# Loading w_ada's columns three steps ahead of their sums in the first pass of an encoder layer

## Chip, cores and metric

The kernel runs on one core of a Trainium2 chip. The metric is the device time of one execution in microseconds (us), lower is better; the median of the runs is compared.

## What is computed

One layer of a gated encoder, 1024 rows by 2048 columns, all in float32:

```python
mod = silu(c) @ w_ada + b_ada                    # w_ada: 2048 x 6144
shift, scale, gate = split(mod, 3)
h = rmsnorm(x, pre_g) * (1 + scale) + shift
q, k, v, gate_a, u, gate_p = split(h @ w_in)     # w_in: 2048 x 4608
y_a = windowed_gqa(q, k, v) * silu(gate_a)
y_p = multiscale_pool(u) * silu(gate_p)
g_a, g_p = split(sigmoid(h @ w_merge + b_merge)) # w_merge: 2048 x 4096
merged = g_a * (y_a @ w_br_attn) + g_p * (y_p @ w_br_pool)
out = x + gate * rmsnorm(merged @ w_out, post_g)
```

The change is about `mod`: a product of one row with a 2048 x 6144 matrix: 50 MB of loads and little arithmetic.

## The kernel before

**The big products.** A column pair is 256 columns of `w_in` or `w_merge`. It is worked out by a seven-product Strassen scheme in `strassen`, with each operand split into a high and a low part (`split`: ScalarE writes `whi`, VectorE writes `wlo`). One product is 12 matmuls of 128x512 on TensorE. The contraction has two halves, so there are two passes over all 34 pairs; the first pass, which the change touches, covers the half of `h` that is made first and stores its partial results in `part_d`.

**Order inside a pair.** `run` puts the last product of a pair behind the second product of the next one. So TensorE's order over a pair is: X (moving operand B11), V (T3), then the last product of the pair before (Z, B22), then Z (T2), X (B21), V (T4), Z (T1). X and V have one PSUM bank each of the tag "mm"; V's bank is read by VectorE after T4 (`finish("21", ...)`, the row `u<-V`), and the next pair's T3 product writes the same bank. The four results of a pair are stored as `c` (block 12 of the pair before, in the middle of the pair), `c` (block 11), `u` (block 21) and `p` (block 22).

**Weights.** Two raw tiles of 512 KB per pair (`load_raws`, line 187; four buffers). The first holds a11 and a21, the second a12 and a22. VectorE makes `ws` = a11 - a21 (L105), then a21 + a22 (`raw<-raw,raw`, L102) and further sums. The low parts `wlo` are ready up to four products ahead, because there are four buffers.

**Side work in the first pass.** The stretch of 22 pairs under `pass1(n1, side, EASY, ...)` carries steps of a deque `side`, alternately four and three steps a pair. In them are the columns 4 to 7 of shift and scale (`modulation_steps`: 32 steps with two 256 KB loads of `w_ada` and two sums on VectorE each, and four closing steps) and then the 32 steps of the gate (`gate_step`: one 512 KB load into a tile shown as `gada`, and one sum into `gacc`). The tiles share a pool `xa` of five buffers. From pair 11 on, `weight_sums` is laid over the same pairs: four loads of `w_out` (tiles `sw`), four sums on VectorE, four stores to `ws_dS`.

**What sets the order.** A scheduler orders each engine's instructions by its own estimates of time, except where `keep` (`keep_in_program_order`) pins an instruction behind the one that was written before it for the same engine. The sums of `weigh` are pinned on VectorE. Every load and store of this stretch goes through SyncE's queue (SP) in one fixed order, and an entry that waits holds up all behind it.

Of the kernel before, what the change touches and what calls it, by code (L numbers as in the profile page):

```python
# [12 lines left out]
F32 = mybir.dt.float32  # L13
# [7 lines left out]
P = 128  # L21
S = 1024
D = 2048
KT = D // P
# [18 lines left out]
def encoder_layer(ctx: ExitStack, tc: tile.TileContext, x, c, table, w_ada, b_ada, pre_g,  # L43
# [18 lines left out]
    w_ada, w_in, w_pg, w_ba, w_bp, w_merge, w_out = (  # L62
        w[0] for w in (w_ada, w_in, w_pg, w_ba, w_bp, w_merge, w_out))

    def pool(name, bufs=1, **kw):
        return tc.tile_pool(name=name, bufs=bufs, reuse_waits="tile", **kw)
# [9 lines left out]
    def uid(s):  # L76
        cnt[0] += 1
        return f"{s}_{cnt[0]}"

    def bank(tag, name="b"):  # L80
        return psum.tile([P, 512], F32, tag=tag, name=uid(name), bufs=1 if tag in SEEDED else 2)
# [8 lines left out]
    def keep(ins):  # L90

        tc.keep_in_program_order(ins)
# [14 lines left out]
    load = nc.sync.dma_start  # L107
# [233 lines left out]
    xa = mid.enter_context(pool("xa", 5))  # L341
# [8 lines left out]
    for r0, src in ((0, c[0]), (16, b_ada[0, 0:D]), (32, b_ada[0, D:2 * D]),  # L350
                    (48, pre_g[0]), (64, b_merge[0]), (96, pool_scale[0])):
        n = src.shape[0] // P
# [60 lines left out]
    def ada_tile(j, q):  # L413
        at = xa.tile([P, 2, 4, P], F32, tag="xa", name=uid("ada"))
        for kk in range(2):
            r0 = (2 * q + kk) * P
            load(at[:, kk].rearrange("p (g h) n -> p g (h n)", g=2), w_ada[r0:r0 + P, 0:2 * D].rearrange("p (g n) -> p g n", g=2)
                 [:, :, j * 256:(j + 1) * 256])
        return at

    def sum_columns(acc):
        pm = bank("at", "PM")
        for g in range(4):
            nc.tensor.matmul(pm[:, g:g + 1], acc[:, g, :], ones, start=True, stop=True)
        return pm

    def mod_columns(j, pm):
        tc.keep_in_program_order(nc.vector.tensor_tensor(
            modc[:, :, :, j], pm[:, 0:4].rearrange("p (g h) -> p g h", g=2),
            cols[:, 16:48].rearrange("p (g k) -> p g k", g=2)[:, :, 2 * j:2 * j + 2], ALU.add))  # L430
        nc.vector.scalar_tensor_tensor(modc[:, 1, :, j], modc[:, 1, :, j], 1.0,
                                       cols[:, 48 + 2 * j:50 + 2 * j], op0=ALU.add, op1=ALU.mult)

    def ada_slots(j):
        tiles = []
        for kc in range(KT):
            tiles.append(slot("ada", F32, (P, 4, P)))
            load(tiles[kc].rearrange("p (g h) n -> p g (h n)", g=2),
                 w_ada[kc * P:(kc + 1) * P, 0:2 * D].rearrange("p (g n) -> p g n", g=2)
                 [:, :, j * 256:(j + 1) * 256])  # L440
        return tiles

    def modulation(j, tile_of, pin=False):

        st_ = {}

        def step(q):
            if q == 0:
                st_["pv"] = bank("at", "GEMV")
            pv = st_["pv"]  # L450
            for kc in (2 * q, 2 * q + 1):
                g = kc % 4 * 32
                ins = nc.tensor.matmul(pv[g:g + 32, :], scz[:, kc, :], tile_of(kc), start=kc < 4,  # L453
                                       stop=kc >= 12, tile_position=(0, g))
                if pin:
                    tc.keep_in_program_order(ins)
            if q == 7:
                acc = xa2.tile([P, 4, P], F32, tag="acc", name=uid("acc"), bufs=2)
                tc.keep_in_program_order(
                    nc.scalar.activation(acc, pv.rearrange("p (g n) -> p g n", g=4), AF.Copy))  # L460
                mod_columns(j, sum_columns(acc))

        return [lambda q=q: step(q) for q in range(8)]

    def weigh(acc, t, kc):

        if kc == 0:
            ins = nc.vector.tensor_scalar(acc, t, sc[:, 0:1], None, op0=ALU.mult)
        else:
            ins = nc.vector.scalar_tensor_tensor(acc, t, sc[:, kc:kc + 1], acc,  # L470
                                                 op0=ALU.mult, op1=ALU.add)
        tc.keep_in_program_order(ins)

    def modulation_steps(j):

        st_ = {}

        def step(q):
            if q == 0:
                st_["acc"] = xa2.tile([P, 4, P], F32, tag="acc", name=uid("acc"), bufs=2)  # L480
            if q == 8:
                mod_columns(j, st_["pm"])
                return
            acc = st_["acc"]
            at = ada_tile(j, q)
            for kk in range(2):
                kc = q * 2 + kk
                weigh(acc, at[:, kk], kc)
            if q == 7:
                st_["pm"] = sum_columns(acc)  # L490

        return [lambda q=q: step(q) for q in range(9)]

    def modulate(eng, t, k):
        j, kh = k // 2, k % 2
# [43 lines left out]
    ada = [ada_slots(0), ada_slots(1)]  # L539
# [11 lines left out]
    side = deque(modulation(2, ada[2].__getitem__, True) + modulation(3, tile3, True))  # L551
# [98 lines left out]
    gp = gate_ctx.enter_context(pool("gatep"))  # L650
    gacc = gp.tile([P, D], F32, name="gacc")

    def gate_step(kc, q):
        qs = slice(q * 1024, (q + 1) * 1024)
        at = xa.tile([P, 1024], F32, tag="xa", name=uid("gada"))
        load(at, w_ada[kc * P:(kc + 1) * P, 2 * D + q * 1024:2 * D + (q + 1) * 1024])
        weigh(gacc[:, qs], at, kc)

    tab = gp.tile([33, NH], F32, name="tab")

# [16 lines left out]
    def gate_columns(n):  # L677
# [16 lines left out]
        else:  # L694
# [6 lines left out]
            nc.scalar.activation(rows, pt[0:KT, 0:P], AF.Copy)  # L701
            store(pg_d.rearrange("o (k p) -> (o k) p", p=P), rows)

    side = deque(s_ for j in range(4, 8) for s_ in modulation_steps(j))
    side.extend(lambda kc=kc, q=q: gate_step(kc, q) for q in range(2) for kc in range(KT))
    side.append(bias_lines)
    side.extend(lambda n=n: gate_columns(n) for n in range(6))
    EASY = ((0, 2, 4, 6), (1, 3, 5))
# [24 lines left out]
    h = {k: [sp.tile([P, 512], F32, name=f"h{k}_{s}") for s in range(2)] for k in PART[1]}  # L733
# [18 lines left out]
    def x_step(n):  # L752
        if n < 2 * NB:
            held[n] = fetch_x(n // 2, n % 2)
        if n >= 2:
            turn_x((n - 2) // 2, n % 2, held.pop(n - 2))

    side = deque(lambda n=n: x_step(n) for n in range(2 * NB + 2))
# [17 lines left out]
    side = deque()  # L776
# [12 lines left out]
    with pool("attn") as ap:  # L789
# [19 lines left out]
        qraw, q, bt, g, pr, pv = {}, {}, {}, {}, {}, {}  # L809
# [230 lines left out]
    for b, w in enumerate((w_ba, w_bp)):  # L1040
# [43 lines left out]
        for i in range(8):  # L1084
# [24 lines left out]
            at = [(n, open_gate) for n in (0, 1, 2, 3)] if i == 0 else []  # L1109
# [175 lines left out]
    side = deque()  # L1285
# [123 lines left out]
```

## Time and profile before

| | us |
|---|---|
| median of three runs | 2145.62 |
| the runs | 2143.08, 2147.35, 2145.62 |
| profiled execution, its own time | 2142.59 |
| its span | 2140.8 |
| TensorE busy in the span | 2096.1 (98%) |
| VectorE busy | 1537.3 (72%) |
| ScalarE busy | 1129.5 (53%) |

The stretch of the first pass with the side steps runs from about 152 us to about 565 us of the span. Times in the timeline rows are counted from the start of the span; a bracket at the end of a row is the idle time of the engine before it and what ended it.

### The profile page before, as it was taken

What the parts mean: (1) busy time and instruction counts of PE and PEld (TensorE: products, weight loads), DVE (VectorE), ACT (ScalarE), POOL (GpSimd) and SP (SyncE); (2) the same over time, 40 slices, a digit from 0 to 9 for tenths busy, and PEclk for the clock granted to TensorE, in tenths of its full rate; (3) what the DMA queues carried; (4) which work ended last, traced back from release to release, by engine and by line L of the source; (5) the groups of instructions that cost most, each with busy time, mean ns of one, the idle gap of its engine ahead of it and who ended that gap; (6) DMA issues with size and microseconds to landing.
All of it is one profiled execution on the core that took longest, in us unless ns stands there. A gap on an engine that the chain in (4) does not pass through costs nothing.

```text
span 2140.8 us, 28950 instructions
## 1 busy us (share of the span) xinstructions
PE 2096.1 (98%) x9567; PEld 1715.2 (80%) x9567; DVE 1537.3 (72%) x2754; ACT 1129.5 (53%) x2124; POOL 7.4 (0%) x66
## 2 busy tenths in 40 slices
PE   6999999999999999999999999999999999999998
PEld 4588888887878888888888888888788888778886
DVE  5786666777547676777776788666956977879667
ACT  5654444443474546767775433333645644667654
POOL 0000000000000000000000000000000000000000
PEclk9999999999999999999999999999999999999999
DMA  9986566898766356445454766765655655696996
GB/s 331 292 277 202 188 207 202 305 315 270 237 216 213 122 169 207 157 156 197 150 165 154 235 214 203 242 193 171 228 170 166 213 192 164 219 298 219 303 306 240
DMA packets 303255, 466.11 MB, mean 218 GB/s; under 512 B 23882, under 2 KB 144866, under 8 KB 303104
## 3 DMA queue, kind: packets, MB, share of 16 engines
q1 hardware_dynamic: 301648, 462.02, 65.6%
q0 software_dynamic: 1120, 2.19, 0.3%
q8 instruction: 75, 1.23, 0.2%
q14 instruction: 76, 0.62, 0.1%
q10 hardware_dynamic: 336, 0.06, 0.0%
HBM read 340.41 MB, written 125.85 MB: 218 GB/s over the span
## 4 chain that ended last, share of the span: by engine, by line
PE 80%; DMA 8%; DVE 7%; issue 2%; ACT 2%; SPq 0%; ACTq 0%; DVEq 0%
PE Z L235 26%; PE V L235 18%; PE X L235 17%; PE Z L1139 2%; PE Z L1141 2%; PE Z L1140 2%; DVE wlo L96 2%; DMA raw<-in_w_merge_dram 1%; PE V L1141 1%; PE V L1139 1%; PE V L1140 1%; PE X L1141 1%; PE X L1140 1%; PE X L1139 1%; PE GEMV L453 1%
## 5 line engine op out<-in xcount | busy, mean ns | idle before, releaser
L95 ACT ACTIVATE whi<-raw 128x512 fp32r<-128x512 f32 (+1 forms) x528 | 319.7, 609 | 504.5 <-PE Z L235 252.6
L96 DVE TENSOR_TENSOR wlo<-raw,whi 128x512 fp32r<-128x512 f32 (+1 forms) x528 | 346.6, 662 | 189.8 <-PE Z L235 116.5
L96 DVE TENSOR_TENSOR wlo<-wr,whi 128x512 fp32r<-128x512 f32 x224 | 151.1, 689 | 60.9 <-ACT whi L95 58.5
L95 ACT ACTIVATE whi<-wr 128x512 fp32r<-128x512 f32 x224 | 138.5, 629 | 92.8 <-DVE wlo L96 35.9
L102 DVE TENSOR_TENSOR raw<-raw,raw 128x512 f32<-128x512 f32 x80 | 55.2, 690 | 94.2 <-DMA raw<-in_w_merge_dram 70.8
L1078 ACT ACTIVATE gt<-gt,cols 128x512 f32<-128x512 f32 x64 | 46.1, 722 | 96.2 <-DMA gt<-proj_d 77.8
L235 PE MATMUL V<-T3h,whi 128*128 128x512 f32 x336 | 92.9, 396 | 3.3 <-DVE u L102 3.3
L235 PE MATMUL X<-B11h,whi 128*128 128x512 f32 x336 | 92.4, 393 | 1.7 <-DVE part L102 0.9
L235 PE MATMUL Z<-B22h,whi 128*128 128x512 f32 x336 | 92.4, 395 | 0.8 <-ACT u L290 0.8
L235 PE MATMUL V<-T4h,whi 128*128 128x512 f32 x336 | 92.0, 393 | 0.4 <-ACT T4h L95 0.4
L235 PE MATMUL Z<-T1h,whi 128*128 128x512 f32 x336 | 91.8, 392 | 0.3 <-ACT T1h L95 0.3
L235 PE MATMUL V<-T3l,whi 128*128 128x512 f32 x336 | 91.5, 392 | 0.0
L235 PE MATMUL Z<-T1l,whi 128*128 128x512 f32 x336 | 91.1, 390 | 0.2
L235 PE MATMUL X<-B11l,whi 128*128 128x512 f32 x336 | 91.1, 390 | 0.2 <-DVE B11l L96 0.2
L235 PE MATMUL Z<-T2h,whi 128*128 128x512 f32 x336 | 91.2, 392 | 0.0
L235 PE MATMUL V<-T4l,whi 128*128 128x512 f32 x336 | 91.0, 390 | 0.0
L235 PE MATMUL X<-B21h,whi 128*128 128x512 f32 x336 | 90.9, 391 | 0.0
L235 PE MATMUL V<-T4h,wlo 128*128 128x512 f32 x336 | 90.8, 390 | 0.0
L235 PE MATMUL Z<-B22l,whi 128*128 128x512 f32 x336 | 90.8, 390 | 0.0
L235 PE MATMUL Z<-T1h,wlo 128*128 128x512 f32 x336 | 90.8, 390 | 0.0
L235 PE MATMUL Z<-T2l,whi 128*128 128x512 f32 x336 | 90.7, 390 | 0.0
L235 PE MATMUL V<-T3h,wlo 128*128 128x512 f32 x336 | 90.6, 390 | 0.0
(306 smaller groups left out, 4847.0 us busy)
## 6 DMA issues: line engine op xcount, KB each, us to landing
part<-part_d SPq DMA_DIRECT2D x136, 256.0 KB, 4.8
ada<-in_w_ada_dram SPq DMA_DIRECT2D x128, 256.0 KB, 4.7
raw<-in_w_in_dram SPq DMA_DIRECT2D x64, 512.0 KB, 4.1
raw<-in_w_merge_dram SPq DMA_DIRECT2D x64, 512.0 KB, 5.7
wr<-ws_dS SPq DMA_DIRECT2D x64, 512.0 KB, 5.3
wr<-in_w_out_dram SPq DMA_DIRECT2D x48, 512.0 KB, 5.0
proj_d<-part SPq DMA_DIRECT2D x68, 256.0 KB, 2.2
sw<-in_w_out_dram SPq DMA_DIRECT2D x64, 256.0 KB, 5.4
```

Source lines behind the costliest of these rows:

```text
L95: ins = (nc.scalar.activation(hi, src, AF.Copy), nc.vector.tensor_tensor(lo, src, f32(hi), ALU.subtract))
L96: nc.vector.tensor_tensor(lo, src, f32(hi), ALU.subtract))
L102: return (eng or nc.vector).tensor_tensor(o, a, b, ALU.add)
L235: nc.tensor.matmul(ps, w_[:, i], op[mov][j][m_], start=fresh and i == 0 and n == 0, stop=i == nj - 1 and n == 2, skip_group_check=True)
L453: ins = nc.tensor.matmul(pv[g:g + 32, :], scz[:, kc, :], tile_of(kc), start=kc < 4, stop=kc >= 12, tile_position=(0, g))
L1078: nc.scalar.activation(gt, gt, AF.Sigmoid, bias=cols[:, col:col + 1])
L1139: nc.tensor.matmul(pb, hi, w[0], start=first, stop=False, skip_group_check=True)
L1140: nc.tensor.matmul(pb, lo, w[0], start=False, stop=False, skip_group_check=True)
L1141: nc.tensor.matmul(pb, hi, w[1], start=False, stop=last, skip_group_check=True)
```

## The change

Each side step of `w_ada` is split into a load and a sum. Step n first does the sum of unit n - 3 and then issues the load of unit n. The 32 + 32 units run through without closing steps of their own (the closing of a column is put ahead of the sum that comes then), so the deque is 74 steps long in place of 75; both make 22 pairs. The loads are pinned with `keep`, the five buffers stay.

```diff
-        def step(q):
+        def load_(q):
+            st_[q] = xa.tile([P, 2, 4, P], F32, tag="xa", name=uid("ada"))
+            for kk in range(2):
+                r0 = (2 * q + kk) * P
+                keep(load(st_[q][:, kk].rearrange("p (g h) n -> p g (h n)", g=2),
+                          w_ada[r0:r0 + P, 0:2 * D].rearrange("p (g n) -> p g n", g=2)
+                          [:, :, j * 256:(j + 1) * 256]))
+
+        def sum_(q):
...
-            acc = st_["acc"]
-            at = ada_tile(j, q)
+            at = st_.pop(q)
             for kk in range(2):
-                kc = q * 2 + kk
-                weigh(acc, at[:, kk], kc)
+                weigh(st_["acc"], at[:, kk], 2 * q + kk)
...
-    def gate_step(kc, q):
-        qs = slice(q * 1024, (q + 1) * 1024)
-        at = xa.tile([P, 1024], F32, tag="xa", name=uid("gada"))
-        load(at, w_ada[kc * P:(kc + 1) * P, 2 * D + q * 1024:2 * D + (q + 1) * 1024])
-        weigh(gacc[:, qs], at, kc)
+    def gate_sum(kc, q):
+        st_ = {}
+
+        def load_():
+            st_["at"] = xa.tile([P, 1024], F32, tag="xa", name=uid("gada"))
+            keep(load(st_["at"], w_ada[kc * P:(kc + 1) * P, 2 * D + q * 1024:2 * D + (q + 1) * 1024]))
+
+        return load_, lambda: weigh(gacc[:, q * 1024:(q + 1) * 1024], st_["at"], kc)
...
-    side = deque(s_ for j in range(4, 8) for s_ in modulation_steps(j))
-    side.extend(lambda kc=kc, q=q: gate_step(kc, q) for q in range(2) for kc in range(KT))
+    AHEAD = 3
+    units, then = [], {}
+    for j in range(4, 8):
+        sums_of, columns = ada_sums(j)
+        units += sums_of
+        then[len(units)] = columns
+    units += [gate_sum(kc, q) for q in range(2) for kc in range(KT)]
+
+    def unit_step(n):
+        m = n - AHEAD
+        if m in then:
+            then[m]()
+        if m >= 0:
+            units[m][1]()
+        if n < len(units):
+            units[n][0]()
+
+    side = deque(lambda n=n: unit_step(n) for n in range(len(units) + AHEAD))
```

The scheduler makes a new order of it on every engine. The first place is late in the gate's steps, on SP, ahead of the first raw tile of the pair that begins at 521 us in the profile before. In the names, `c` is a partial result on its way to `part_d`, `raw` a raw weight tile, `sw` and `ws_dS` belong to the weight sums. Before:

```order
L656 DMA gada_4567<-in_w_ada_dram 128x1024
L656 DMA gada_4610<-in_w_ada_dram 128x1024
L656 DMA gada_4661<-in_w_ada_dram 128x1024
L656 DMA gada_4716<-in_w_ada_dram 128x1024
L311 DMA part_d<-c_4487 128x512
L187 DMA raw_4657<-in_w_merge_dram 128x4x256
L656 DMA gada_4757<-in_w_ada_dram 128x1024
L311 DMA part_d<-c_4545 128x512
```

And after, ahead of the first raw tile of the same pair (here `raw_4666`):

```order
L661 DMA gada_4430<-in_w_ada_dram 128x1024
L661 DMA gada_4478<-in_w_ada_dram 128x1024
L187 DMA raw_4505<-in_w_merge_dram 128x4x256
L636 DMA sw_4527<-in_w_out_dram 128x512
L636 DMA sw_4529<-in_w_out_dram 128x512
L636 DMA sw_4531<-in_w_out_dram 128x512
L311 DMA part_d<-c_4496 128x512
L636 DMA sw_4533<-in_w_out_dram 128x512
L661 DMA gada_4536<-in_w_ada_dram 128x1024
L187 DMA raw_4666<-in_w_merge_dram 128x4x256
```

Four gate loads in a row have become one or two at a time.

The second place is VectorE around the read of V's bank (`u<-V`) at the same point. Before, the difference `ws` of the following pair, which needs its first raw tile, stands ahead of that read:

```order
L96 TENSOR_TENSOR wlo_4616<-ws_4613,whi_4615 128x512
L105 TENSOR_TENSOR sw_4520<-sw_4518,sw_4520 128x512
L105 TENSOR_TENSOR ws_4780<-raw_4657 128x512
L105 TENSOR_TENSOR sw_4633<-sw_4522,sw_4520 128x512
L102 TENSOR_TENSOR sw_4518<-sw_4518,sw_4633 128x512
L102 TENSOR_TENSOR u_964_4516<-V_4425,u_964_4516 128x512
L470 TENSOR_SCALAR gacc<-gada_4567,sc,gacc 128x1024
```

After, that difference comes eight rows behind the read, and all four weight sums stand ahead of it:

```order
L96 TENSOR_TENSOR wlo_4625<-ws_4622,whi_4624 128x512
L105 TENSOR_TENSOR sw_4529<-sw_4527,sw_4529 128x512
L105 TENSOR_TENSOR sw_4642<-sw_4531,sw_4529 128x512
L102 TENSOR_TENSOR sw_4527<-sw_4527,sw_4642 128x512
L105 TENSOR_TENSOR sw_4533<-sw_4533,sw_4642 128x512
L102 TENSOR_TENSOR u_968_4525<-V_4434,u_968_4525 128x512
L470 TENSOR_SCALAR gacc<-gada_4430,sc,gacc 128x1024
L96 TENSOR_TENSOR wlo_4648<-raw_4343,whi_4647 128x512
```

The wait for a raw tile has left the rows ahead of the read; a wait for the weight sums' loads may stand there instead.

The third place is SP two pairs earlier, where the four loads of a weight-sum unit are issued. Before, all four are ahead of the store of block 12:

```order
L633 DMA sw_4157<-in_w_out_dram 128x512
L633 DMA sw_4159<-in_w_out_dram 128x512
L633 DMA sw_4161<-in_w_out_dram 128x512
L633 DMA sw_4163<-in_w_out_dram 128x512
L656 DMA gada_4336<-in_w_ada_dram 128x1024
L311 DMA part_d<-c_4154 128x512
L187 DMA raw_4332<-in_w_merge_dram 128x4x256
```

After, three of them are behind it:

```order
L661 DMA gada_4145<-in_w_ada_dram 128x1024
L636 DMA sw_4166<-in_w_out_dram 128x512
L311 DMA part_d<-c_4163 128x512
L636 DMA sw_4168<-in_w_out_dram 128x512
L636 DMA sw_4170<-in_w_out_dram 128x512
L636 DMA sw_4172<-in_w_out_dram 128x512
L661 DMA gada_4199<-in_w_ada_dram 128x1024
```

The loads of the weight sums have moved back by up to a store; the four sums that use them stand ahead of `u<-V` on VectorE there too.

More of the change, by code (lines that the diff above doesn't have):

```diff
@@ L472, in weigh, with ada_sums @@
         tc.keep_in_program_order(ins)
-    def modulation_steps(j):
+    def ada_sums(j):
         st_ = {}
-        def step(q):
+        def load_(q):
[6 more added lines that the diff above has]
+        def sum_(q):
             if q == 0:
                 st_["acc"] = xa2.tile([P, 4, P], F32, tag="acc", name=uid("acc"), bufs=2)
-            if q == 8:
-                mod_columns(j, st_["pm"])
-                return
-            acc = st_["acc"]
-            at = ada_tile(j, q)
+            at = st_.pop(q)
             for kk in range(2):
-                kc = q * 2 + kk
-                weigh(acc, at[:, kk], kc)
+                weigh(st_["acc"], at[:, kk], 2 * q + kk)
             if q == 7:
-                st_["pm"] = sum_columns(acc)
-        return [lambda q=q: step(q) for q in range(9)]
+                st_["pm"] = sum_columns(st_["acc"])
+        return [(lambda q=q: load_(q), lambda q=q: sum_(q)) for q in range(8)], lambda: mod_columns(j, st_["pm"])
     def modulate(eng, t, k):
```

## The prediction

> **What bounds the kernel now.** I read the page's first part, then the stretch table for this pass, then TensorE's waits in it.
>
> ```profile
> span 2140.8 us, 28950 instructions
> PE 2096.1 (98%) x9567; PEld 1715.2 (80%) x9567; DVE 1537.3 (72%) x2754; ACT 1129.5 (53%) x2124; POOL 7.4 (0%) x66
> ```
>
> TensorE is busy in 98% of the span, so the change can only bring what TensorE loses in the stretch that it touches. The stretch table (busy us and count for each engine, then granted clock, share of the DMA engines, GB/s) and TensorE's waits between 140 and 570 us:
>
> ```profile
> 100.00:150.00 50.00, 50.00 (x222) 41.42 (x221) 42.54 (x91) 30.28 (x65) 0.10 (x1) 1.00 0.85 282
> 400.00:510.00 110.00, 107.54 (x469) 88.58 (x468) 82.71 (x116) 43.96 (x73) 0.00 (x0) 0.98 0.90 305
> PE V L235 <- DVE u L102: 2.5, 1, 2.5
> ```
>
> One wait in the whole stretch: a T3 product waits until VectorE has read V's bank. Its neighbourhood on TensorE (start, duration, instruction; the first rows of three pairs and the T3 product of two):
>
> ```profile
> 478.97 1.07 PE L235 MATMUL X<-B11h,whi 128*128 128x512 f32 x4
> 481.69 0.62 PE L235 MATMUL V<-T3h,whi 128*128 128x512 f32 x2
> ...
> 498.01 1.07 PE L235 MATMUL X<-B11h,whi 128*128 128x512 f32 x4
> 503.35 2.08 PE L235 MATMUL V<-T3h,whi 128*128 128x512 f32 x4 [2.46 <-DVE u L102]
> 505.23 1.72 PE L235 MATMUL V<-T3l,whi 128*128 128x512 f32 x4
> 506.78 1.09 PE L235 MATMUL V<-T3h,wlo 128*128 128x512 f32 x4
> ...
> 521.32 0.84 PE L235 MATMUL X<-B11h,whi 128*128 128x512 f32 x3
> ```
>
> An undisturbed pair lasts 498.01 - 478.97 = 19.04 us, the disturbed one 521.32 - 498.01 = 23.31: the stall costs 4.27 us, more than the bracket says. T3 begins 5.34 us into the pair in place of 481.69 - 478.97 = 2.72, so 2.62 are waiting. The other 1.65 are slower matmuls: four in 2.08 and 1.72 us, against 1.07 to 1.09 elsewhere. The clock rows say why:
>
> ```profile
> 490.00:500.00 10.00, 10.00 (x46) 8.29 (x45) 5.58 (x9) 3.69 (x6) 0.00 (x0) 1.00 0.95 337
> 500.00:505.00 5.00, 2.54 (x8) 1.76 (x8) 4.29 (x6) 1.21 (x2) 0.00 (x0) 0.82 0.71 266
> 505.00:510.00 5.00, 5.00 (x21) 3.99 (x20) 4.97 (x8) 1.45 (x3) 0.00 (x0) 0.84 0.75 230
> ```
>
> The granted clock falls from 1.00 to 0.82 and 0.84 for these 10 us. Where VectorE's lateness is from, on VectorE and on SP:
>
> ```profile
> 494.93 0.68 DVE L105 TENSOR_TENSOR sw<-sw,sw 128x512 f32<-128x512 f32 x1
> 500.68 0.69 DVE L105 TENSOR_TENSOR ws<-raw 128x512 f32<-128x512 f32 x1 [5.07 <-DMA raw<-in_w_merge_dram]
> 501.29 0.68 DVE L105 TENSOR_TENSOR sw<-sw,sw 128x512 f32<-128x512 f32 x1
> 502.62 0.68 DVE L102 TENSOR_TENSOR u<-V,u 128x512 f32<-128x512 f32 x1
> ...
> 484.57 5.27 SPq L656 DMA_DIRECT2D gada<-in_w_ada_dram  x4
> 489.93 0.41 SPq L311 DMA_DIRECT2D part_d<-c  x1
> 493.11 0.38 SPq L187 DMA_DIRECT2D raw<-in_w_merge_dram  x1
> ```
>
> Four gate loads leave SP together, the raw tile leaves at 493.11 and lands some 7.5 us later, and VectorE stands 5.07 us before `ws`, with `u<-V` three rows behind. It was near this limit before:
>
> ```profile
> 442.30 0.68 DVE L102 TENSOR_TENSOR u<-V,u 128x512 f32<-128x512 f32 x1
> 461.32 0.68 DVE L102 TENSOR_TENSOR u<-V,u 128x512 f32<-128x512 f32 x1
> 480.56 0.69 DVE L102 TENSOR_TENSOR u<-V,u 128x512 f32<-128x512 f32 x1
> ```
>
> The third ends at 481.25, T3 starts at 481.69: 0.44 us to spare. The other two end at 442.98 and 462.00; with T3 every 19.04 us, at 443.61 and 462.65, they had 0.6 us. So this is a queue of pairs that runs at its limit while the gate's loads, the weight sums and the raw tiles share DMA engines that are 0.90 busy.
>
> **The change part by part.** *The number of steps* goes from 75 to 74; at 3.5 steps a pair both need 22 pairs, so TensorE's work is the same: nothing.
>
> *The loads that leave the stage before.* By SP's order, ten 256 KB loads of w_ada for these sums went out in the stage before the 22 pairs; now all but two or three come later. TensorE was busy 50.00 of 50 us between 100 and 150 (row above), so the freed DMA time buys nothing: nothing, and if a wait there were hidden in the busy time, a gain below 1 us.
>
> *SP's waits for buffers.* SP's own waits in the stretch:
>
> ```profile
> SPq L417 <- DVE acc L470: 25.6, 24, 3.0
> SPq L656 <- DVE gacc L470: 6.4, 3, 3.7
> ```
>
> A load now goes out when the sum of five units before is already two steps old, so these 32 us of head-of-queue waiting mostly go. By themselves they are worth nothing: SP is not on TensorE's path, except through the raw tiles. That is the next term.
>
> *The stall at 500 us.* With `ws` behind `u<-V`, a raw tile that lands at +1.5 us of the next pair no longer holds V's bank. What is late next is the four weight sums and the raw tiles' sum a21 + a22, which in three pairs also stands ahead of `u<-V`. I followed VectorE's new order pair by pair with these rows:
>
> ```profile
> gada<-in_w_ada_dram SPq DMA_DIRECT2D x28, 512.0 KB, 7.6
> raw<-in_w_merge_dram SPq DMA_DIRECT2D x12, 512.0 KB, 6.7
> sw<-in_w_out_dram SPq DMA_DIRECT2D x32, 256.0 KB, 5.6
> DMA to landing us min/median/max: 2.5/5.5/7.9
> 510.64 0.60 ACT L308 ACTIVATE c<-Z 128x512 f32<-128x512 f32 x1 [0.23 <-PE Z L235]
> ```
>
> (the first three: KB each, median us to landing between 340 and 510 us; the fourth: of the `sw` transfers from 380 to 510.) A VectorE row follows the last after some 0.61 us, a gate sum after 1.2. `u<-V` can start after T4, 6 x 2.72 = 16.3 us into the pair, and has to end by 19.04 + 2.72 = 21.76. Three cases occur. Where a21 + a22 stands ahead, its tile is issued behind the store of block 12, at 3 x 2.72 + 0.60 + about 0.6 = 9.4; it lands at 16.1, and with four rows `u<-V` ends at 18.5. Where the weight sums stand ahead and their last load goes out at about 12 (third place of the order), it lands at 17.6, and the last sum and `u<-V` end at 18.8. Elsewhere nothing is waited for, 17.1. Each is about 3 us inside the limit, where before three pairs in a row were 0.4 to 0.6 us inside and the fourth outside. So I take the whole 4.27 us as gone. Bounds: 0 (another wait takes its place) and 4.27 for this stall.
>
> *The closing matmuls of a column.* Four small matmuls (PM, L424) wait on TensorE for the last sum of a column. In one of four places they now stand right behind T3, 5.44 us into a pair, and the last sum is the fourth of a group that stood at the same place of VectorE's order in an earlier column:
>
> ```profile
> 209.17 1.07 PE L235 MATMUL X<-B11h,whi 128*128 128x512 f32 x4
> ...
> 213.97 0.74 DVE L470 SCALAR_TENSOR_TENSOR acc<-ada,sc,acc 128x512 f32<-128x512 f32 x1
> ```
>
> It ended at 214.71, 5.54 us into the pair, so TensorE waits 0.1 us, or up to 0.9 where the raw tile's sum ahead of it comes later. I take 0.3, since the row is near the lower end.
>
> *Sum.* 4.27 - 0.3 = 4.0 us of gain. Against the profiled execution's own time (2142.59, span 2140.8 and 1.79 around it): 2138.6. That execution is 3.0 us below the median of the runs, 2145.62, against which the sum gives 2141.6. The runs lie 2147.35 - 2143.08 = 4.27 us apart, the price of one stall, and three pairs stand 0.4 to 0.6 us before one; I take half of the 3.0 us as stalls of this stretch that go too: **2140.1 us**, 0.26% below the median. About 0.2% (4.3 us) is what a measurement of this kernel can tell from no change.
>
> **The rivals.** *Only the waiting comes back.* The clock fell after a wait of 2.46 us, in stretches that did not line up with the wait; if it dips elsewhere in the new program anyway, only 2.62 - 0.3 = 2.3 us are gained: 2143.3, no difference to be told. [...]
>
> *One stall stays or moves.* For it: the DMA engines are 0.90 busy and the change moves the same bytes. Then 2145.62 + 0.3 = 2145.9. Against it: the 3 us of room.
>
> *The weight sums become the gate (slower).* In three pairs all four weight sums stand ahead of `u<-V` while loads of theirs are issued behind the store of block 12 (third place of the order). Each time the last load, issued at about 12 us, needs longer than 21.76 - 1.2 - 12 = 8.5 us, T3 waits. The longest landing of these tiles was 7.9 in the stretch. If three pairs stall at 4.27 each with the old one gone: 2145.62 - 4.0 + 12.8 = 2154.4; with two, 2150.2. For it: the row is 0.6 us from the deciding point, and SP may come later than 12 to these loads, since it passes stores that wait. Against it: median 5.5.
>
> **How the numbers follow.** Stall gone: 0.57, its own range 2138 to 2142.2; of it 0.43 is below 2141.3, the 0.2% line, and 0.14 above. Only the waiting: 0.08, same. One stall stays: 0.15, same. Weight sums: 0.20, slower by over 0.2%. So faster 0.43, same 0.37, slower 0.20. Range 2137.5 to 2150.5: it holds the first three cases and the two-stall half of the last, and leaves out about 0.1 above and 0.05 below.
>
> **What would show it.** In the profile after: no wait of TensorE on `DVE u` between 340 and 530 us and the clock at 1.00 there; every pair without small matmuls at 19.04 us; `u<-V` ending 17 to 19 us into its pair; SP's waits of L482 and L661 on `acc` and `gacc` near nothing; gate loads one or two at a time. The prediction is wrong if a T3 product still waits for `u<-V`, if VectorE stands before `sw` or `raw` for 5 us with that read behind it, or if PM waits more than 1 us on TensorE.

## The result, and the profile after

| | before | after |
|---|---|---|
| median of 19 runs each, us | 2146.33 (2142.49 to 2152.86) | 2140.43 (2136.79 to 2146.99) |
| profiled execution, its own time | 2142.59 | 2139.16 |
| ratio of the times | 1 | 0.9974, 95% interval 0.9965 to 0.9983 |

The changed kernel is faster by 0.26%, which is 5.6 us (3.6 to 7.5). The forecast was 2140.1 us. The first rows of the page after:

```profile
span 2137.3 us, 28934 instructions
PE 2094.5 (98%) x9567; PEld 1713.6 (80%) x9567; DVE 1537.4 (72%) x2754; ACT 1129.1 (53%) x2124; POOL 7.4 (0%) x66
```

TensorE is busy 1.6 us less and the span is 3.5 us shorter: part of the gain is that matmuls run faster, part that TensorE waits less. The stretch table after, for the same windows as in the prediction, and then TensorE's only wait between 140 and 700 us:

```profile
400.00:510.00 110.00, 110.00 (x487) 91.10 (x486) 87.54 (x123) 46.03 (x76) 0.00 (x0) 1.00 0.93 315
500.00:505.00 5.00, 5.00 (x23) 4.13 (x23) 5.00 (x6) 2.44 (x4) 0.00 (x0) 1.00 1.00 342
505.00:510.00 5.00, 5.00 (x23) 4.13 (x22) 5.00 (x8) 2.11 (x4) 0.00 (x0) 1.00 0.91 292
PE b L767 <- ACT xt L761: 2.9, 2, 1.7
```

The wait on `DVE u` is gone, the clock is 1.00 where it was 0.82 and 0.84, and the DMA engines are busier than before (0.93 for 0.90, 315 GB/s for 305): loads that left in the stage before now come later (between 100 and 150 us the rate fell from 282 to 257 GB/s). (The wait that is left belongs to the next part of the program, and was 4.1 us before.) For the whole stretch I use one row of the stretch table for each kernel, from the X product at 152 us to the X product nineteen pairs later: before, after, and the kernel before in a second profiled execution (run e12):

```profile
152.37:521.32 368.95, 366.40 (x1623) 302.88 (x1622) 257.00 (x383) 151.78 (x247) 0.00 (x0) 1.00 0.72 241
152.82:517.72 364.90, 364.77 (x1624) 301.74 (x1622) 260.26 (x388) 151.71 (x247) 0.66 (x1) 1.00 0.76 250
153.04:523.76 370.72, 366.81 (x1623) 302.73 (x1622) 256.50 (x382) 151.82 (x247) 0.00 (x0) 1.00 0.73 239
```

The first number behind the window is its length, the second TensorE's busy time in it. The stretch takes 368.95 and 370.72 us before, 364.90 after. TensorE waits 2.55 and 3.91 us in it before, and 0.13 after.

How close VectorE comes to the limit after, in its worst pair (VectorE's rows; X of this pair starts at 479.64, the next T3 at 501.40):

```profile
494.06 0.69 DVE L102 TENSOR_TENSOR raw<-raw,raw 128x512 f32<-128x512 f32 x1 [3.04 <-DMA raw<-in_w_merge_dram]
494.67 0.69 DVE L96 TENSOR_TENSOR wlo<-raw,whi 128x512 fp32r<-128x512 f32 x1
...
496.60 1.41 DVE L105 TENSOR_TENSOR sw<-sw,sw 128x512 f32<-128x512 f32 x2
...
499.26 0.68 DVE L102 TENSOR_TENSOR u<-V,u 128x512 f32<-128x512 f32 x1
```

A wait for a raw tile still stands ahead of `u<-V`, now before a21 + a22, and the four weight sums stand ahead of it too. It ends at 499.94, 1.46 us inside the limit. (In the second trace of the changed kernel, e5, the same pair has 2.54 us.)

### The profile page after: what moved, and what is told of

It is laid out like the page before. It is cut to its first block, busy times and chain, and to the rows that moved or that the text cites. A ratio compares the mean times of both kernels' runs of the same rounds, so it can differ in the third digit from the quotient of the medians.

```text
span 2137.3 us, 28934 instructions
## 1 busy us (share of the span) xinstructions
PE 2094.5 (98%) x9567; PEld 1713.6 (80%) x9567; DVE 1537.4 (72%) x2754; ACT 1129.1 (53%) x2124; POOL 7.4 (0%) x66
## 4 chain that ended last, share of the span: by engine, by line
PE 86%; DVE 6%; DMA 5%; ACT 1%; issue 1%; SPq 0%; ACTq 0%; DVEq 0%; POOLq 0%
PE Z L235 29%; PE V L235 19%; PE X L235 19%; PE Z L1161 2%; PE Z L1162 2%; PE Z L1163 2%; PE V L1161 1%; PE V L1163 1%; PE V L1162 1%; PE GEMV L453 1%; PE X L1163 1%; DVE wlo L96 1%; PE X L1162 1%; PE X L1161 1%; PE PT L894 1%
## 5 line engine op out<-in xcount | busy, mean ns | idle before, releaser
L102 DVE TENSOR_TENSOR u<-V,u 128x512 f32<-128x512 f32 x94 | 64.5, 687 | 37.3 <-PE V L235 36.7
```

What stands on the lines that cost most here:

```text
L102: return (eng or nc.vector).tensor_tensor(o, a, b, ALU.add)
```

## The experiments

The theory that I took to the chip: on VectorE `ws` of the next pair stands ahead of `u<-V`; when its raw tile is late, `u<-V` is late, V's bank stays taken and T3 waits. Rivals for the cause: the bunch of gate loads alone, the pins, the lead alone, the full DMA engines alone, the modulation half of the change, or chance in one execution. The stretch column is the length just shown, the next one the length from the same X to the X three pairs further on (22 pairs, 152.37 to 584.00 us in the kernel before), the DMA column the share of the DMA engines between 360 and 520 us.

| kernel | stretch, us | 22 pairs, us | DMA | time over before, 95% interval |
|---|---|---|---|---|
| before, first profile | 368.95 | 431.6 | 0.87 | 1 |
| before again (e12) | 370.7 | 433.8 | 0.87 | 0.9994 (0.9977 to 1.0010) |
| after | 364.9 | 427.6 | 0.92 | 0.9974 (0.9965 to 0.9983) |
| after again (e5) | 365.0 | 427.6 | 0.92 | 0.9974 (0.9964 to 0.9985) |
| pins only (e1) | 372.7 | 444.4 | 0.90 | 1.0052 (1.0038 to 1.0066) |
| lead only (e2) | 365.0 | 427.7 | 0.89 | 0.9988 (0.9978 to 0.9998) |
| gate loads only (e3) | 367.1 | 429.9 | 0.92 | 0.9988 (0.9977 to 1.0000) |
| modulation loads only (e4) | 368.9 | 431.6 | 0.89 | 1.0006 (0.9995 to 1.0018) |
| before, weight sums from stage 14 (e6) | 368.9 | 433.4 | 0.78 | 0.9973 (0.9963 to 0.9984) |
| after, weight sums from stage 14 (e7) | 365.8 | 431.1 | 0.79 | 0.9995 (0.9985 to 1.0006) |
| before, `ws` on GpSimd (e9) | 364.9 | 427.6 | 0.90 | 1.0077 (1.0057 to 1.0098) |
| after, lead of one step (e10) | 367.2 | 431.5 | 0.95 | 1.0001 (0.9988 to 1.0014) |
| before, weight sums from stage 35 (e11) | 365.1 | 427.8 | 0.79 | 0.9976 (0.9964 to 0.9988) |
| after, with copies of X (e8), one run | 367.2 | 429.8 | 0.90 | 2159.54 us, no interval |

The 22 pairs go with the times better than the stretch does, since some kernels lose their gain just behind it. Against the first profile of the kernel before, e1 is 12.7 us longer over them; e4, e7 and e10 are 0 to 0.6 us shorter, e3 is 1.7 and e2, e11 and both traces of after are 3.9 to 4.1. Three kernels don't fit. e8 has a single run, and e9 loses its time in a later pair, as shown below. e6 is 1.7 us longer over these pairs and yet 0.27% faster; that stays open.

**Both kernels again.** Unaltered, so there is no edit.

> The changed kernel once more, unaltered: a second profiled execution and more times, as the measure for what one trace can tell. If the gain is the order of the instructions, the stretch from 140 to 570 us again has no PE wait and 19.04 us pairs, X of the 30th pair again starts some 3.6 us earlier than in the kernel before, and the ratio is again 0.9965 to 0.9983. If the gap of the first traces was chance of one execution, pairs over 19.04 us show up between 360 and 520 us.

> The kernel before once more, unaltered: a second profiled execution. If the stall belongs to the order of its instructions, a pair of 22 to 24 us with a PE wait on u<-V shows near 498 us again. [...] The prediction took half of the 3.0 us between the median and the profiled execution for further stalls of this kind: then a second pair over 19.04 us shows between 360 and 500 us.

The second trace of after has the same stretch to 0.1 us and no PE wait. The second trace of before has the stall in the same place and another one two pairs earlier (TensorE's rows; X of the two pairs starts at 460.59 and 500.21):

```profile
464.72 1.19 PE L235 MATMUL V<-T3h,whi 128*128 128x512 f32 x4 [1.25 <-DVE u L102]
...
505.67 1.20 PE L235 MATMUL V<-T3h,whi 128*128 128x512 f32 x4 [2.57 <-DVE u L102]
506.70 1.56 PE L235 MATMUL V<-T3l,whi 128*128 128x512 f32 x4
```

These pairs last 20.59 and 23.55 us instead of 19.04. The stretch of this execution is 370.72 - 364.9 = 5.8 us longer than after, about what the times differ by. The total says less: the two of after differ by 4.6 us in their own time (2139.16 and 2143.73) with equal stretches. The difference arises later; two pairs at 601 to 651 us alone last 47.0 and 49.6 us. TensorE waits for `xt` there in both traces (1.66 and 2.29 us at 636 us), but only in e5 does a stretch of half clock follow, from 636.63 to 640.04 us (the granted clock over 601 to 651 us is 0.97 in e5 and 1.00 in the first trace). The kernel before has none there in its first trace (1.00). So two executions of one kernel can differ by such a stretch; the part on the price of a stall comes back to it.

**Halves of the change.** Pins only (kernel before, a load still directly ahead of its sum):

```diff
-        load(at, w_ada[kc * P:(kc + 1) * P, 2 * D + q * 1024:2 * D + (q + 1) * 1024])
+        keep(load(at, w_ada[kc * P:(kc + 1) * P, 2 * D + q * 1024:2 * D + (q + 1) * 1024]))
```

and the same around the modulation loads.

> The kernel before, with its loads of w_ada pinned in SP's order but still directly in front of their sums; 75 steps as before. Theory (the stall came from four gate loads that left SP together and made the raw tile late for the ws that stands ahead of u<-V): gate loads leave one or two at a time, no PE wait on u<-V between 140 and 570 us, no pair of 23.3 us, so at least the 4.27 us of the stall come back: 0.9980 of the time before, and 0.9974 if the rest of the gain hangs on it too. Rival (the lead of three steps carries the gain): VectorE waits for each load to land, sums and u<-V run late, and the time is that of before, 1.000, or longer.

It is 0.52% slower, so the rival was right and I was wrong. The gate loads do leave one or two at a time, and the stall isn't gone. TensorE's waits from 140 to 570 us, and VectorE's on gate loads from 152 to 570 us:

```profile
PE V L235 <- DVE u L102: 6.5, 5, 2.4
PE X L235 <- DVE wlo L96: 2.4, 1, 2.4
PE PM L426 <- DVE acc L472: 2.4, 4, 0.9
DVE gacc L472 <- DMA gada<-in_w_ada_dram: 27.6, 17, 3.8
DVE gacc L470 <- DMA gada<-in_w_ada_dram: 1.4, 1, 1.4
```

Before, the scheduler had itself put these loads ahead of their sums (VectorE waited 1.9 us for them in all). The pin takes that away, and VectorE waits 29.0 us for loads issued just ahead of their sums. The stretch is only 3.7 us longer than in the first profile of before; most of the loss lies in the pair that begins at 548.05 us, which lasts 29.88 us in place of 22.71. Lead only (the changed kernel without pins):

```diff
-            keep(load(st_["at"], w_ada[...]))
+            load(st_["at"], w_ada[...])
```

> The changed kernel without the pins on its w_ada loads, three steps of lead kept. SP's order then still sends gate loads in bunches of three, but ws stands behind u<-V in most pairs of the gate's stretch. Theory (bunched loads make the raw tile late): the stall stays in some form, one pair of over 21 us with a PE wait on u<-V, 0.999 to 1.000 of the time before. Rival (the place of ws ahead of u<-V on VectorE decides, the bunches alone do nothing): no PE wait on u<-V, 0.9974 to 0.998.

The gate loads still leave in bunches, yet there is no PE wait from 140 to 570 us, and the stretch is as short as after. My theory of the bunches fell, though they are of two and three here (e9 below has the four): `ws` stands behind `u<-V` in most pairs. The ratio of 0.9988 is short of after's 0.9974, with overlapping intervals; the stretch doesn't show a difference, so what the pins add to the lead stays open. Lead of one step, pinned:

```diff
-    AHEAD = 3
+    AHEAD = 1
```

> The changed kernel with a lead of one step instead of three, loads pinned. With no lead (pin only) VectorE waited 27.6 us in 17 sums for gate loads and the time was 1.0052 of before. If a step (some 5 us) covers a load's landing of 4 to 8 us only in part: waits of VectorE on gate loads of some 10 us, 0.998 to 1.001 of the time before. If what counts is that the order of the sums behind u<-V changes, not the landing: as the changed kernel, 0.997 to 0.998.

VectorE still waits 21.1 us for gate loads, twice what I had guessed:

```profile
DVE gacc L470 <- DMA gada<-in_w_ada_dram: 16.4, 14, 3.5
DVE gacc L468 <- DMA gada<-in_w_ada_dram: 4.7, 2, 4.0
```

So with pins and a lead of 0, 1 and 3 steps VectorE waits 29.0, 21.1 and 0 us for gate loads, and the ratio is 1.0052, 1.0001 and 0.9974: in this kernel a pinned load needs the lead. How VectorE's waits reach TensorE in e10 isn't shown; TensorE's own waits up to 570 us are only 0.7 us on a PM product and 0.8 on the gate's transpose.

**Gate or modulation.** The edit splits the new deque in two; the other half keeps its old steps.

```diff
+    units = [gate_sum(kc, q) for q in range(2) for kc in range(KT)]
...
+    mods = [s_ for j in range(4, 8) for s_ in modulation_steps(j)]
```

> Only the gate's 32 loads are moved ahead and pinned; the modulation steps are as before. Theory (all of the gain lies in the gate's stretch): the stall goes, 0.9974 to 0.998 of the time before. Rival (the modulation loads that left the stretch before, or their sums, give part of it): less than that, 0.999.

> Only the modulation's 32 steps (two loads each) are moved ahead and pinned; the gate's loads are as before. Theory: the gate's four loads still leave together, the pair of 23.3 us is there, 1.000 of the time before within 0.001. Rival: 0.999 or less, without a change in the stall.

The modulation half alone changes nothing and keeps the stall (2.2 us of waiting, a pair of 23.01). The gate half takes the large stall away but has two waits of 0.9 us in the same stretch:

```profile
PE Z L235 <- ACT u L245: 0.9, 1, 0.9
PE V L235 <- DVE u L102: 0.9, 1, 0.9
```

Its order on VectorE is that of after in the gate's steps; its raw tiles were issued up to 2.4 us later into the pair. So the room after is thin enough that the modulation half's order takes part in it.

**The link itself.** In the kernel before, only the engine of `ws` is changed:

```diff
-            sub(s3, a11, a21)
+            if part is None and nj == 4:
+                nc.gpsimd.tensor_tensor(s3, a11, a21, ALU.subtract)
+            else:
+                sub(s3, a11, a21)
```

> The kernel before; only ws (a11 less a21) of the first pass's 41 whole pairs is taken on GpSimd instead of VectorE. SP's order is that of before (gate loads in threes and fours), VectorE's too, with the ws rows gone, so u<-V no longer stands behind the raw tile. Theory (VectorE's wait for raw ahead of u<-V is what makes PE wait): no PE wait on u<-V between 340 and 530 us although raw lands as late as before, the 30th pair's X some 4 us earlier, 0.998 of the time before. Rival (the late raw tile delays the weights anyway, through a21+a22 or through ws and its weights): a pair of over 21 us stays, with a PE wait on wlo or whi instead, 1.000. A subtraction on GpSimd that is much longer than VectorE's 0.69 us could cost waits of its own in every pair: then slower than before.

Up to this place the orders on SP and (without the `ws` rows) on VectorE are those of before, four gate loads leave together as before, and the DMA engines are 0.90 busy, but TensorE doesn't wait once (SP's, GpSimd's and VectorE's rows, then the stretch table):

```profile
484.45 5.27 SPq L659 DMA_DIRECT2D gada<-in_w_ada_dram  x4
493.00 0.38 SPq L187 DMA_DIRECT2D raw<-in_w_merge_dram  x1
500.13 1.48 POOL L261 TENSOR_TENSOR ws<-raw 128x512 f32<-128x512 f32 x1 [18.77 <-DMA raw<-in_w_merge_dram]
498.58 0.68 DVE L102 TENSOR_TENSOR u<-V,u 128x512 f32<-128x512 f32 x1
360.00:520.00 160.00, 160.00 (x708) 132.48 (x707) 124.10 (x166) 66.78 (x109) 13.06 (x9) 1.00 0.90 301
```

`u<-V` runs while `ws` still waits for its raw tile. The raw tile also leaves earlier, 11.5 us into its pair (X at 481.45) in place of 14.1 before. SP shows why: the store of `u` stands ahead of the raw tile, so a late `u<-V` makes the next raw tile later, from pair to pair (store issued at 481.28 before, 2.3 us into the next pair, and at 479.65 here, 1.8 us before its end). The tile of e9 so lands 0.36 us before the next X (500.49), and e9 alone doesn't separate the place of `ws` from the earlier tile. This kernel is slower for another reason: in a new order of TensorE, one pair at 582 us lasts 53.81 us, with transposes between its products and a granted clock of 0.71.

The changed kernel itself separates them. In the kernel before, the tile that stalled T3 landed 500.68 - 498.01 = 2.67 us into a pair. In the changed kernel one landed later still, 483.00 - 479.64 = 3.36 us into a pair, and T3 did not wait for VectorE, because `u<-V` stood ahead of `ws` and had run by then (VectorE's rows of the changed kernel):

```profile
479.56 0.68 DVE L102 TENSOR_TENSOR u<-V,u 128x512 f32<-128x512 f32 x1
...
483.00 0.69 DVE L105 TENSOR_TENSOR ws<-raw 128x512 f32<-128x512 f32 x1 [2.15 <-DMA raw<-in_w_merge_dram]
```

In e5 the same tile landed 2.92 us into the pair, again without a wait of TensorE.

**The DMA engines.** The eleven weight sums are spread over more of the pass:

```diff
-    pass1(n1, side, EASY, lay_out(11, 70, 7 * n1 - 2))
+    pass1(n1, side, EASY, lay_out(11, 14, 7 * n1 - 2))
```

> The kernel before; only the eleven weight sums of the first pass (loads of 1 MB and stores of 1 MB each) are laid from stage 14 on instead of stage 70, so that fewer of them share the DMA engines with the gate's loads. The gate's loads still leave SP in threes and fours, and ws still stands ahead of u<-V in every pair. Theory (the raw tile is late because the DMA engines are full, order only makes it hurt): raw tiles land sooner, no T3 stall, 0.998 of the time before or better. Rival (bunch and order on VectorE suffice): a pair of over 21 us with a PE wait on u<-V stays, 1.000.

> The changed kernel with the same spread of the weight sums. If what is left of the gain was lost to full DMA engines, 0.9965 of the time before or less; if the changed kernel has nothing left to lose there, the same as the changed kernel, 0.997 to 0.998. The sums now stand among the modulation's steps, where they could make a PM product wait: then 0.998 to 1.000.

With 35 in place of 14:

> The kernel before with the weight sums laid from stage 35 on (spread from stage 14 gave 0.9973 with a new 2.7 us wait of a PM product at 293 us in its trace, and no T3 stall). If the DMA share of the gate's stretch is what counts and the PM wait is an accident of stage 14, no stall of either kind: 0.995 to 0.997, better than the changed kernel. If the share is not low enough from stage 35, the T3 stall is back: 0.999 to 1.000.

In e11, `ws` stands ahead of `u<-V` as before, gate loads leave in threes, and there is no stall: the stretch is 365.1 and the ratio that of after. So either half of the cause suffices to break it: raw tiles that land in time, or `ws` out of the way. In e6 the same mechanism struck elsewhere, in a column's last sum (VectorE's and TensorE's rows):

```profile
292.06 0.69 DVE L102 TENSOR_TENSOR raw<-raw,raw 128x512 f32<-128x512 f32 x1 [2.54 <-DMA raw<-in_w_in_dram]
293.94 0.75 DVE L470 SCALAR_TENSOR_TENSOR acc<-ada,sc,acc 128x512 f32<-128x512 f32 x1
294.83 1.02 PE L424 MATMUL PM<-ones,acc 128*128 128x1 f32 x8 [2.72 <-DVE acc L470]
```

That pair lasted 24.49 us. Why e6's times are nevertheless as good as after's I can't say from one trace; it may not wait there in every execution. e7 got a 1.0 us PM wait, a 1.4 us wait of the gate's transpose and a pair of 24.55 at 540 us (21.93 in after), and most of the gain is lost. No version beat the changed kernel: e6 and e11 equal it, and none of these effects add up.

**The price of a stall.** Sixteen pairs of the changed kernel get more copies of X on ScalarE:

```diff
-        nc.scalar.activation(bz, bx, AF.Copy)
+        for _ in range(1 + EXTRA.get(pairs_[0], 0)):
+            nc.scalar.activation(bz, bx, AF.Copy)
```

> The changed kernel with stalls of known size put in: in sixteen pairs ScalarE copies X to Z 6 to 11 times in a row instead of once (0.58 us each; the result is the same), so that the T2 product waits for it about 0.8, 1.3, 1.9, 2.5, 3.1 or 3.7 us. By the prediction's row (a wait of 2.46 us brought one window of 3.413 us at half clock, and with it 1.65 us) waits of 2.5 us and more each cost 1.7 us above the wait, shorter ones nothing. [...]

Most of the stalls didn't come: the scheduler knows the copies and put T4's products into the gap. Over the whole program TensorE waited for these copies six times, 5.5 us in all:

```profile
PE Z L235 <- ACT Z L274: 5.5, 6, 2.5
```

The longest was 2.5 us. The one run took 2159.54 us, which these waits explain only in part. The rest of the answer is in the other traces. In the first trace of before, two stretches of half clock lie ahead of the program's last microseconds. Each lasts 3.413 us, and they begin 471.04 us apart (at 32.12 and 503.16 us), which is 138 times that length; two of pins only, shown further down, begin 17.07 us apart (at 553.10 and 570.17 us), five times. Rows of the stretch table in windows of that length: before (two windows), pins only (two), modulation only (two), before again (two), and before once more, further on (two):

```profile
499.75:503.16 3.41, 1.14 (x6) 0.60 (x4) 2.45 (x4) 1.21 (x2) 0.00 (x0) 1.00 0.57 222
503.16:506.57 3.41, 3.22 (x8) 2.55 (x9) 3.41 (x5) 0.00 (x0) 0.00 (x0) 0.50 0.84 256
...
467.77:471.18 3.41, 1.61 (x7) 1.35 (x8) 3.41 (x5) 0.02 (x1) 0.00 (x0) 1.00 0.77 263
471.18:474.59 3.41, 3.41 (x17) 2.82 (x16) 2.00 (x4) 1.38 (x3) 0.00 (x0) 1.00 0.92 291
...
499.58:502.99 3.41, 1.46 (x7) 0.88 (x5) 2.42 (x4) 1.21 (x2) 0.00 (x0) 1.00 0.74 285
502.99:506.40 3.41, 3.19 (x8) 2.53 (x9) 3.41 (x5) 0.00 (x0) 0.00 (x0) 0.50 0.88 251
...
503.68:507.09 3.41, 1.42 (x6) 1.20 (x7) 3.38 (x6) 0.03 (x1) 0.00 (x0) 1.00 0.72 271
507.09:510.50 3.41, 3.41 (x10) 2.64 (x9) 3.41 (x5) 1.12 (x2) 0.00 (x0) 0.50 0.88 231
...
636.28:639.69 3.41, 1.52 (x7) 0.94 (x5) 0.00 (x0) 0.05 (x1) 0.00 (x0) 1.00 0.99 314
639.69:643.10 3.41, 2.68 (x14) 2.30 (x15) 1.39 (x2) 3.17 (x9) 0.00 (x0) 1.00 0.87 272
```

Where TensorE was busy for 1.14, 1.42 or 1.46 us of such a window, the next ran at half clock (column with 0.50). After 1.52 and 1.61 us it ran at full clock. The length of the wait did not give the price: 2.40 us of waiting in e1, 0.6 us of it ahead of 467.77 and 1.8 behind, cost its pair 2.71 us (21.75 in place of 19.04) with the clock at 1.00, and 2.46 us before cost 4.27. That is 0.31 and 1.81 us above the wait, where the expectation of e8 took 1.7 from 2.5 us on and nothing below. The two traces of after above go with these rows: the window ahead held 1.75 us of matmul in the first trace (633.03 to 636.44), with full clock behind it, and 1.13 in e5 (633.21 to 636.63), with half clock. But the busy time does not sort all windows. In the first trace of before half clock also followed 1.68 us (28.70 to 32.12), and in pins only it followed two windows with more (each with the window behind it; then the row that they share):

```profile
549.69:553.10 3.41, 2.25 (x15) 1.97 (x14) 1.56 (x3) 1.21 (x2) 0.00 (x0) 1.00 0.94 307
553.10:556.51 3.41, 3.41 (x9) 2.64 (x9) 3.34 (x6) 0.00 (x0) 0.00 (x0) 0.50 0.83 281
566.76:570.17 3.41, 2.04 (x13) 1.86 (x14) 3.35 (x6) 1.23 (x2) 0.00 (x0) 1.00 0.47 177
570.17:573.58 3.41, 3.41 (x9) 2.63 (x9) 1.74 (x3) 0.00 (x0) 0.00 (x0) 0.50 0.93 292
...
550.77 0.95 PE L694 MATMUL GATE<-ones,gacc 128*128 128x1 f32 x8
569.17 0.95 PE L694 MATMUL GATE<-ones,gacc 128*128 128x1 f32 x8
```

Both hold eight gate matmuls with one column of output, 0.95 us, and 1.3 and 1.1 us without them. Whether these matmuls are the reason isn't shown, nor is a limit of busy time below which the clock falls.

## Why the prediction was right, by its steps

- **The stall is gone, 4.27 us.** Right. The pairs that begin at 479.64 and 498.68 after last 19.04 us, and the stretch is 368.95 - 364.90 = 4.05 us shorter between the first two traces, for a forecast of 4.0. That `ws` ahead of `u<-V` is the link was argued then; the raw tile that landed 3.36 us into its pair without harm shows it, and e9 and e2 agree. That four loads leave together was named beside it; breaking them up isn't needed for the cure (e9 still sends four together, e2 and e11 three).
- **Half of the 3.0 us between median and profiled execution as further stalls, 1.5.** This was the least founded term. One execution now bears it out: e12 has a second stall, of 20.59 - 19.04 = 1.55 us, in a pair that ended `u<-V` 0.6 us inside the limit in the first trace. How often it comes isn't known from two traces. The scatter from which the term was taken did not shrink with the change (10.4 us from the fastest to the slowest of 19 runs before, 10.2 after), so that the forecast met the median to 0.3 us is in part luck.
- **The closing matmuls, 0.3.** The four pairs with PM last 20.23, 20.28, 19.99 and 20.07 after, 19.99, 19.99, 20.32 and 20.05 before: 0.2 us more in all.
- **The steps, and the loads that left the stage before: nothing.** X of the stretch's first pair starts at 152.82 and 152.54 in the two traces after, at 152.37 and 153.04 in those before. Nothing can be told.
- **SP's waits for buffers.** They went (L482 and L661 wait 0.5 and 0.2 us for `acc` and `gacc` in the stretch, where it was 25.6 and 6.4), and SP sends the gate loads one or two at a time.
- **The room of 3 us.** This term was mis-sized. For a21 + a22 ahead of `u<-V` the working was good: a tile issued 9.4 us into the pair, and `u<-V` ending at 17.7 to 18.4 for 18.5, in the pairs at 365, 384 and 403 us. For the weight sums it gave 18.8, and three pairs in a row ended at 19.0, 19.6 and 20.3. I had costed the raw tile and the weight sums as separate cases; in the pair shown above they stand one behind the other. The room was 1.46 us in this trace (2.37 in the tightest pair of e5), half of what I counted on, and e3 shows that a raw tile issued some 2 us later already stalls.
- **Only the waiting comes back (the clock).** Not in this case: the clock has no dip in the stretch after (1.00). But the 1.65 us that I added to the wait is no fixed price. A wait of 2.40 us in e1 cost 2.71, at a clock of 1.00, and the one of 2.46 us before cost 4.27, with 3.413 us at half clock behind it.
- **The weight sums become the gate.** No T3 wait on them. The nearest pair had 1.46 us left, so a chance of 0.20 was not too much.

## What to carry to other kernels

A load that was pinned directly ahead of its use cost more here than one that the scheduler could move (VectorE waited 29.0 us for gate loads in e1 and 1.9 before): pin it only with a lead longer than its landing under load (6.0 us in the median after, 7.2 at most; a lead of one step left 21.1 us of waiting, three steps none). When a bottleneck engine waits for a short operation, look one row up on the engine that does it: here it waited behind work for the next pair, and moving that row or making its tile arrive sooner each cured it, while doing both brought nothing more. Work out the room of the worst case with all the waits in one queue, not each by itself, and compare one stretch between traces instead of the whole span, long enough to hold every pair that the edit can reach.

## What the hardware showed

Two stretches of half clock in the first trace of before lasted 3.413 us each, and began 138 such lengths apart. Of the windows of that length above, those with 1.14, 1.42 and 1.46 us of matmul were followed by half clock and those with 1.52, 1.61 and 1.75 by full clock, but half clock also followed 1.68 us before, and 2.04 and 2.25 in pins only; what sets these apart stays open. A wait of about 2.5 us had two prices, 2.7 us (e1) and 4.3 (before). A subtraction of 128x512 took 1.67 us on GpSimd in the mean of 46 (e9; 1.48 in the row above) and 0.69 on VectorE.
